# A decoder MLP in split float32: operand rows loaded in place, part sums left in two tiles, another order at the stage changes

## The chip, the core and the metric

The kernel runs on one core of a Trainium2 chip. The metric is device time in microseconds, the median of several executions; one further execution was profiled, and every row below comes from that one. The engines: TensorE (PE, the matrix engine), VectorE (DVE), ScalarE (ACT), GpSimd (POOL) and SyncE (SP). Here SP only issues DMAs, and POOL after the first third of the kernel does nothing else either.

## The reference, cut to what is computed

One layer of a decoder over 576 rows (512 prompt rows and 8x8 sample rows). The part that the change touches is the second half, `finish_layer`:

```python
D_MODEL = 2048; D_FF = 4 * D_MODEL
def finish_layer(x, attn, conv_y, pe, ...):
    ...
    x = x + jnp.concatenate([attn, conv_y], axis=-1) @ w_out
    hid = jnp.square(jax.nn.relu(rms_norm(x, g_mlp) @ w_up))
    x = x + hid @ w_down
    gate = jax.nn.sigmoid(rms_norm(x, g_ple) @ w_ple_gate)
    return x + (pe @ w_ple) * gate
```

All of it is float32. The kernel splits each operand into a high part in a shorter format (`float32r`) and a low part, the rest, and makes a product from three matmuls: high by high, high by low, low by high.

## The kernel before

**Layout and stages.** Features lie on the 128 partitions, rows along the free axis (`NR` = 576, `HR` = 288 is half). The first 925 us are the input projection, attention and convolution, which the change leaves alone. Then come the output projection (`outproj`, 16 tiles of 96 matmuls), the up projection, the down projection, the gate and a short end.

**The quad.** Up, down and gate run over *quads*: one 256x256 block of weights against one slot of operands. Up and down use a fast 2x2 block product: 7 products in place of 8 (`PRODS`), each of three matmuls of 288 columns, so 21 matmuls in a quad (lines 1415 to 1421). The order of the products in a quad is 0, 5, 6, 4, 1, 2, 3, and each has a PSUM bank of its own (`pr[i]`); of the eight banks one is spare, so a new segment's second product needs the bank of the old segment's product 0, its third that of product 5, and so on.

**Weights.** `QStream` loads two quads' weights at a time (`w2r`, 512 KB, three buffers, on SP's queue), DVE makes three block sums of them (lines 1613 to 1615), ACT rounds the seven blocks to the high part (`w2h`) and DVE subtracts for the low part (`w2l`), three buffers each. `prep(q)` is called two quads ahead. On DVE the first block sum of the *next* load stands ahead of this quad's `w2l`.

**Operand slots.** A slot holds the seven operand blocks of 128x288 in high and low form (`xs`: `[128, 2, 7, 288]`, a ring of eight). The raw blocks lie in DRAM (`up_in`, `down_in`, tensors `ui` and `di`); `slot_loads` fetches them in two DMAs (432 and 576 KB) into the two buffers of a staging tile `ro`, and `slot` lets ACT write the high part from `ro` and DVE the low part. The slots 0, 1 and 7 of the up projection are made straight from the output projection (`split7`).

**Segments.** A segment is one output tile's run of quads. Up has 32 segments of 8 quads. Down goes in rounds over its 8 output tiles (`plan`): in the first round the tiles take 3, 3, 3, 4, 5, 6, 7 and 8 quads, later 7 each. After a segment the seven products are combined to the tile `c` (`combine_head`, `combine_tail`: 2 copies on ACT, 6 operations on DVE). A down segment that isn't the tile's last one adds its `c` to `x1` in DRAM by an accumulating DMA from POOL (line 1290). `c` has two buffers. `fin_up` scales, applies ReLU and squares an up tile, makes its blocks (`tsums`) and stores them to `down_in`.

**What sets the order.** The engines' programs are in the order in which the code writes them. `Beside` holds two queues of generators that do the work beside the matmuls: queue 0 the finishing work (`fins`), queue 1 the slots. `run` steps them on a credit in us per quad, with queue 0 ahead of queue 1; `flush` and `flush_all` force them. `mk(g, j)` puts the making of slot j on queue 1; a table of hooks calls it at the quad after which the slot's place in the ring was last read.

**Ahead of the up projection.** Before the first quad the code flushes slots 2, 3 and 4 (`bg.flush(slots[1, j].work)`), so their splits stand on ACT and DVE ahead of the weights of quad 2. `prep(0)` and `prep(1)` were called in the last tile of the output projection. `fin_out(p)` finishes a pair of output projection tiles: scaled copy `cg`, blocks `T`, the stores to `up_in`, and then the squares for the norm (`sq`); `cg`, `T` and `sq` share two buffers (tag `b`).

## Time and profile before

| What | Value |
|---|---|
| median of 3 runs | 2873.62 us (2868.43 to 2873.94) |
| profiled execution, its time | 2875.02 us |
| profiled execution, its span | 2873.2 us |
| PE busy | 2730.2 us (95%) |
| DVE busy | 2061.0 us (72%) |
| ACT busy | 1176.8 us (41%) |
| mean granted TensorE clock | 0.978 |
| HBM read and written | 431.53 MB and 95.55 MB |

How to read the rows that follow. A row of the windows view names a stretch in us from the span's start and gives its length, then for PE, PEld (the weight load), DVE, ACT and POOL the busy time with the number of instructions in brackets, then the granted TensorE clock, the share of the DMA engines that was busy, and GB/s. A timeline row has start, duration, engine, line, operation, output and inputs, and in square brackets the idle time ahead of it with what ended that wait. Matmuls are pipelined, so one lasts about 0.29 us while the next starts 0.13 us later. A group row gives count, busy time and mean ns of one. A waits row gives total, times and longest.

### The profile page before, as it was taken

To read this page: it belongs to the slowest core of one execution; us is meant where nothing else is said; L and a number is where in the kernel's file an instruction comes from. 1 tells how busy PE (TensorE), PEld (TensorE's weight loads), DVE (VectorE), ACT (ScalarE), POOL (GpSimd) and SP (SyncE) were. 2 spreads that over 40 slices of the span, in tenths; PEclk is the share of its full clock that TensorE was granted. 3 is DMA by queue.
4 is the path that set the end of the run, shared out by engine and by line. 5 is a ranking of instruction groups with operands and counts; after the bars stand their busy time and mean duration, and the time that the engine had idled before them with its cause. 6 is when DMAs were issued, how large, how long until landed. Compare 5 with 4: busy or idle time off the path is not lost.

```text
span 2873.2 us, 56874 instructions
## 1 busy us (share of the span) xinstructions
PE 2730.2 (95%) x22165; PEld 2624.0 (91%) x22165; DVE 2061.0 (72%) x3613; ACT 1176.8 (41%) x1755; POOL 396.0 (14%) x702
## 2 busy tenths in 40 slices
PE   7999999999999998899999999989999999998996
PEld 7888888898787997899999999989999999998996
DVE  5577766766644434788888888888887888897444
ACT  4232233345633323444444444444444444444332
POOL 1167755741100000000000000000000000000000
PEclk9999999999999999999999999999999999999998
DMA  4599888988745444444444444466665656555445
GB/s 147 173 276 288 268 276 267 286 279 299 257 140 173 145 159 160 129 136 138 141 147 144 137 135 145 154 193 185 159 184 144 180 163 175 167 178 182 156 149 176
DMA packets 243536, 530.81 MB, mean 185 GB/s; under 512 B 25793, under 2 KB 31170, under 8 KB 243266
## 3 DMA queue, kind: packets, MB, share of 16 engines
q1 hardware_dynamic: 197330, 422.72, 45.5%
q10 hardware_dynamic: 33552, 60.87, 7.1%
q0 software_dynamic: 12384, 43.58, 6.5%
q8 instruction: 174, 2.85, 0.4%
q14 instruction: 96, 0.79, 0.1%
HBM read 431.53 MB, written 95.55 MB: 183 GB/s over the span
## 4 chain that ended last, share of the span: by engine, by line
PE 63%; DVE 5%; DMA 3%; ACT 2%; issue 2%; SPq 0%; DVEq 0%; ACTq 0%
PE P L1420 16%; PE P L1419 16%; PE P L1421 15%; PE U L463 7%; PE P L1458 2%; PE P L1460 2%; PE P L1459 2%; PE U L1074 1%; DVE w2l L152 1%; DMA ro<-di 1%; DMA ui<-cg 1%; ACT xs L149 1%; DMA ro<-ui 1%; DVE xs L152 0%; ACT sq L1215 0%
## 5 line engine op out<-in xcount | busy, mean ns | idle before, releaser
L1419 PE MATMUL P<-xs,w2h 128*128 128x288 f32 x3584 | 1069.1, 298 | 35.7 <-ACT w2h L149 11.3
L1420 PE MATMUL P<-xs,w2h 128*128 128x288 f32 x3584 | 1068.1, 298 | 4.0 <-DVE xs L152 4.0
L1421 PE MATMUL P<-xs,w2l 128*128 128x288 f32 x3584 | 1064.5, 297 | 6.0 <-DVE w2l L152 6.0
L149 ACT ACTIVATE w2h<-w2r 128x896 fp32r<-128x896 f32 (+1 forms) x576 | 523.3, 915 | 771.8 <-PE P L1420 471.1
L152 DVE TENSOR_TENSOR w2l<-w2r,w2h 128x896 fp32r<-128x896 f32 (+1 forms) x576 | 600.3, 1042 | 175.8 <-ACT w2h L149 174.0
L1419 PEld LDWEIGHTS P<-xs,w2h 128*128 128x128 f32 x3584 | 680.9, 190 | 42.2 <-ACT w2h L149 11.8
L1421 PEld LDWEIGHTS P<-xs,w2l 128*128 128x128 f32 x3584 | 680.0, 190 | 7.9 <-DVE w2l L152 7.8
L1420 PEld LDWEIGHTS P<-xs,w2h 128*128 128x128 f32 x3584 | 681.9, 190 | 5.5 <-DVE xs L152 5.2
L463 PE MATMUL U<-xh,whi 128*128 128x288 f32 x1792 | 405.1, 308 | 11.0 <-ACT whi L123 10.1
L463 PE MATMUL U<-xh,wlo 128*128 128x288 f32 x1792 | 387.5, 298 | 9.2 <-DVE wlo L129 9.2
L463 PE MATMUL U<-xl,whi 128*128 128x288 f32 x1792 | 386.7, 298 | 2.3 <-DVE xl L298 1.2
L463 PEld LDWEIGHTS U<-xh,whi 128*128 128x128 f32 x1792 | 291.1, 191 | 32.7 <-issue 17.1
L463 PEld LDWEIGHTS U<-xh,wlo 128*128 128x128 f32 x1792 | 291.1, 190 | 11.1 <-DVE wlo L129 11.1
L463 PEld LDWEIGHTS U<-xl,whi 128*128 128x128 f32 x1792 | 291.2, 191 | 3.2 <-DVE xl L298 1.7
L123 ACT ACTIVATE whi<-wraw 128x512 fp32r<-128x512 f32 x224 | 141.0, 630 | 295.0 <-PE U L463 162.6
L1290 POOL DMA_DIRECT2D x<-c x32 | 27.6, 861 | 1565.9 <-DVE c L1531 1565.9
L129 DVE TENSOR_TENSOR wlo<-wraw,whi 128x512 fp32r<-128x512 f32 x224 | 159.3, 712 | 113.0 <-ACT whi L123 110.3
L1613 DVE TENSOR_TENSOR w2r<-w2r 128x512 f32<-128x512 f32 (+1 forms) x272 | 177.9, 654 | 48.7 <-DMA w2r<-in_w_up 24.9
L984 DVE SCALAR_TENSOR_TENSOR y<-ue,cv,y 128x512 f32<-128x512 f32 x240 | 183.4, 764 | 4.2
L985 POOL TENSOR_SCALAR cvt<-us,cv 128x64 f32<-128x64 f32 x240 | 166.5, 694 | 21.6
L1458 PE MATMUL P<-xs,w2h 128*128 128x288 f32 x512 | 152.8, 298 | 0.1
L1459 PE MATMUL P<-xs,w2h 128*128 128x288 f32 x512 | 152.4, 298 | 0.0
(331 smaller groups left out, 2981.6 us busy)
## 6 DMA issues: line engine op xcount, KB each, us to landing
k<-in_cache_kv SPq DMA_DIRECT2D x256, 256.0 KB, 5.2
v<-in_cache_kv SPq DMA_DIRECT2D x256, 256.0 KB, 5.0
w2r<-in_w_up SPq DMA_DIRECT2D x128, 512.0 KB, 4.0
w2r<-in_w_down SPq DMA_DIRECT2D x112, 512.0 KB, 4.3
wraw<-in_w_main ACTq DMA_DIRECT2D x160, 256.0 KB, 5.4
di<-T SPq DMA_DIRECT2D x32, 576.0 KB, 4.2
ro<-di SPq DMA_DIRECT2D x32, 576.0 KB, 5.6
x<-c POOLq DMA_DIRECT2D x32, 576.0 KB, 6.1
```

The lines of the kernel that those rows point to most:

```text
L129: self.nc.vector.tensor_tensor(lo, self.raw.pop(c), f(hi), ALU.subtract)
L149: self.nc.scalar.activation(out, in_, AF.Copy, **kw)
L152: self.nc.vector.tensor_tensor(out, in_, f(hi), ALU.subtract)
L463: self.nc.tensor.matmul(u[:, r, :HR], w, x[:, r * HR:(r + 1) * HR], start=first and n == 0, stop=last and n == 2)
L984: nc.vector.scalar_tensor_tensor(y, ue[:, j:j + NPR], w, y, ALU.mult, ALU.add)
L985: nc.gpsimd.tensor_scalar(t, us[:, :, j:j + 8], w, None, ALU.mult)
L1419: nc.tensor.matmul(o, hi[:, ia, :], s.hi[:, ib, :], start=(k == k0), stop=False)
L1420: nc.tensor.matmul(o, hi[:, ia, :], s.lo[:, ib, :], start=False, stop=False)
L1421: nc.tensor.matmul(o, lo[:, ia, :], s.hi[:, ib, :], start=False, stop=(k == k1 - 1))
L1458: nc.tensor.matmul(o, hi[:, ia, :], s.hi[:, kh, rows], start=first and kh == 0, stop=False)
L1459: nc.tensor.matmul(o, hi[:, ia, :], s.lo[:, kh, rows], start=False, stop=False)
L1613: lambda: V(w[:, :, 4:6, :], w[:, :, 0:1, :].broadcast_to([128, m, 2, 128]), w[:, :, 1:3, :], ALU.add),
```

## The change

It does five things.

1. **Slots load in place.** For up and down, `mk` now issues one DMA (128x2016, all seven blocks) into the low half of the slot itself, at once and not when the slot's work is reached; `slot` rounds from there to the high half and subtracts in place. The gate's slots do the same within their work. Only slot 2 of the up projection still comes through `ro` (`slot_early`).
2. **Part sums leave in two tiles.** A down segment that isn't a tile's last makes `c` without the products 1, 2 and 3 (`part_head`: one copy on ACT, four operations on DVE), and ACT copies those three products to a tile `e` (`part_tail`). POOL adds `e` to `x1` and then `c`.
3. **First up segment.** Slots 2 to 6 are no longer flushed ahead of the first quad but one each after quads 0 to 4; three weight loads and `prep(0)` to `prep(2)` stand in the last output projection tile, where two stood.
4. **`fin_out`** writes the squares ahead of the operands (except for the last pair).
5. **First gate segment**: queue 0 isn't flushed one quad before its end any more, only at the end.

**Where rows move.** First ACT, from the end of the output projection into the up projection (`whi` are output projection weights, `w2h` the new weights, `xs` slots, `cg` and `T` the last output pair). Before:

```order
L123 ACTIVATE whi<-wraw 128x512 x4
L149 ACTIVATE w2h<-w2r 128x896 x2
L149 ACTIVATE xs<-ro 128x864
L149 ACTIVATE xs<-ro 128x1152
L149 ACTIVATE xs<-ro 128x864
L149 ACTIVATE xs<-ro 128x1152
L149 ACTIVATE xs<-ro 128x864
L149 ACTIVATE xs<-ro 128x1152
L149 ACTIVATE w2h<-w2r 128x896 x2
L1237 ACTIVATE cg<-c,vecs 128x576 x2
```

and now:

```order
L123 ACTIVATE whi<-wraw 128x512 x4
L149 ACTIVATE w2h<-w2r 128x896 x3
L1236 ACTIVATE cg<-c,vecs 128x576 x2
L149 ACTIVATE xs<-cg 128x288
L149 ACTIVATE xs<-cg 128x576
L149 ACTIVATE xs<-T 128x1152
L149 ACTIVATE xs<-ro 128x864
L149 ACTIVATE xs<-ro 128x1152
L149 ACTIVATE w2h<-w2r 128x896
L149 ACTIVATE xs<-xs 128x864
L149 ACTIVATE xs<-xs 128x1152
```

The weights of the third quad moved ahead of all slots, the last output pair ahead of slot 2, and between two slots there is now one quad's weights.

Second, DVE at the same place (`wlo` is the low part of output projection weights, `w2r` the block sums, `c<-U,rx` the eviction of an output projection tile). Before:

```order
L1118 TENSOR_TENSOR c<-U,rx 128x576
L129 TENSOR_TENSOR wlo<-wraw,whi 128x512 x2
L1613 TENSOR_TENSOR w2r<-w2r 128x2x256
L1614 TENSOR_TENSOR w2r<-w2r 128x2x128
L1615 TENSOR_TENSOR w2r<-w2r 128x2x128
L1613 TENSOR_TENSOR w2r<-w2r 128x2x256
L152 TENSOR_TENSOR w2l<-w2r,w2h 128x896
L1614 TENSOR_TENSOR w2r<-w2r 128x2x128
L1615 TENSOR_TENSOR w2r<-w2r 128x2x128
L152 TENSOR_TENSOR w2l<-w2r,w2h 128x896
L1118 TENSOR_TENSOR c<-U,rx 128x576
```

and now:

```order
L1117 TENSOR_TENSOR c<-U,rx 128x576
L129 TENSOR_TENSOR wlo<-wraw,whi 128x512
L1653 TENSOR_TENSOR w2r<-w2r 128x2x256
L1654 TENSOR_TENSOR w2r<-w2r 128x2x128
L1655 TENSOR_TENSOR w2r<-w2r 128x2x128
L1653 TENSOR_TENSOR w2r<-w2r 128x2x256
L152 TENSOR_TENSOR w2l<-w2r,w2h 128x896
L1654 TENSOR_TENSOR w2r<-w2r 128x2x128
L129 TENSOR_TENSOR wlo<-wraw,whi 128x512
L1655 TENSOR_TENSOR w2r<-w2r 128x2x128
L152 TENSOR_TENSOR w2l<-w2r,w2h 128x896
L1653 TENSOR_TENSOR w2r<-w2r 128x2x256
```

The last `wlo` of the output projection moved behind the sums of the first two weight loads.

Third, SP from the last up segment into the down projection (`di_126` and so on are the raw blocks of one slot each, `di_153` the store of an up tile, 512 or 2x512 a load of one or two quads' weights). Before:

```order
L1598 DMA w2r<-in_w_down 128x2x512
L1246 DMA di_153<-c 128x288
L1247 DMA di_153<-c 128x576
L1248 DMA di_153<-T 128x1152
L1493 DMA ro<-di_123 128x864
L1493 DMA ro<-di_123 128x1152
L1598 DMA w2r<-in_w_down 128x512
L1493 DMA ro<-di_124 128x864
L1493 DMA ro<-di_124 128x1152
L1598 DMA w2r<-in_w_down 128x2x512
L1493 DMA ro<-di_125 128x864
L1493 DMA ro<-di_125 128x1152
```

and now, behind the slots `di_123` to `di_125` and the first two quads' weights:

```order
L1247 DMA di_153<-T 128x1152
L1345 DMA xs<-di_126 128x2016
L1638 DMA w2r<-in_w_down 128x512
L1345 DMA xs<-di_127 128x2016
L1345 DMA xs<-di_128 128x2016
L1638 DMA w2r<-in_w_down 128x2x512
L1345 DMA xs<-di_129 128x2016
L1345 DMA xs<-di_130 128x2016
L1638 DMA w2r<-in_w_down 128x512
L1638 DMA w2r<-in_w_down 128x2x512
```

All eight slots' loads now stand within the last up segment, one per quad, with the weights of the third quad behind four of them and those of the sixth behind all eight.

**The diff:**

```diff
@@ -184,7 +184,6 @@
 
     heads = 0
     draining = False
-    loaded = None
     later = []
 
 
@@ -1133,12 +1132,12 @@
             for _ in gen:
                 bg.spend(EL(512) / 2)
                 if n == KT - 1 and h == 0:
-                    self.W.dma(0)
-                    self.W.dma(1)
+                    for i in range(3):
+                        self.W.dma(i)
                 if n == KT - 1 and h == 5:
-                    self.loaded = self.slot_loads(self.up_in[2])
-                if n == KT - 1 and h in (4, 6):
-                    bg.spend(self.W.prep(h // 2 - 2))
+                    self.early = self.slot_early(self.up_in[2])
+                if n == KT - 1 and h in (2, 4, 6):
+                    bg.spend(self.W.prep(h // 2 - 1))
                 bg.run(8 * n + h, 1.6)
                 h += 1
             if n % 2 and n < KT - 1:
@@ -1250,6 +1249,8 @@
     def fin_out(self, p, c):
         nc = self.nc
         nc.sync.dma_start(self.x1[p], c)
+        if p < 7:
+            yield from self.squares(p, c)
         cg, T = yield from self.operands(c, self.g_mlp[:, 2 * p:2 * p + 2])
         if p in (0, 1, 7):
             s = self.xslot() if p < 2 else self.last
@@ -1258,8 +1259,8 @@
             h.hi, h.lo = s[:, 0], s[:, 1]
         else:
             self.stored(cg, T, self.up_in[p])
-        yield from self.squares(p, c)
         if p == 7:
+            yield from self.squares(p, c)
             yield from self.norm(self.P_)
 
     def phase2(self):
@@ -1287,6 +1288,9 @@
         def fin_down(p, c, r, final):
 
             if not final:
+                c, e = c
+                quarters = self.x1[p].rearrange("p a (b n) -> p (a b) n", b=2)
+                nc.gpsimd.dma_start(quarters[:, :3, :], e[:, :3, :], accum_op=ALU.add)
                 nc.gpsimd.dma_start(self.x1[p], c, accum_op=ALU.add)
                 yield 0
                 return
@@ -1326,27 +1330,37 @@
         segs, W, slots, fin_of = self.segs, self.W, self.slots, self.fin_of
         fins = (None, fin_up, fin_down, fin_gate)
 
-        def mk(g, j, s=None):
+        def mk(g, j, early=None):
 
             h = slots[g, j] = Slot()
+            t = self.xslot()
+            h.hi, h.lo = t[:, 0], t[:, 1]
+            src = (self.up_in, self.down_in, self.x2)[g - 1][j]
+            if g == 3:
+                h.hi, h.lo = (x.rearrange("p a n -> p (a n)")[:, :2 * NR].rearrange("p (a n) -> p a n", a=2)
+                              for x in (h.hi, h.lo))
+
+            def load():
+                bg.flush(fin_of[g - 1, j])
+                nc.sync.dma_start(f(h.lo), src)
+
+            if g < 3 and not early:
+                load()
 
             def build():
-                bg.flush(fin_of[g - 1, j])
-                t = s or self.xslot()
-                h.hi, h.lo = t[:, 0], t[:, 1]
+                if g == 3:
+                    load()
+                if not early:
+                    yield -2
                 if g < 3:
-                    yield from self.slot(t, (self.up_in, self.down_in)[g - 1][j], EL)
+                    yield from self.slot(t, early)
                     return
-                h.hi, h.lo = (x.rearrange("p a n -> p (a n)")[:, :2 * NR].rearrange("p (a n) -> p a n", a=2)
-                              for x in (t[:, 0], t[:, 1]))
-                r = t2.tile([128, 2, NR], F32, name="ro", tag="ro", bufs=2)
-                nc.sync.dma_start(r, self.x2[j])
-                yield -2
                 for i in range(2):
                     gv = self.g_ple[:, 2 * j + i:2 * j + i + 1]
-                    self.split_hi(h.hi[:, i, :], r[:, i, :], scale=gv)
-                    nc.vector.scalar_tensor_tensor(h.lo[:, i, :], r[:, i, :], gv, f(h.hi[:, i, :]), ALU.mult, ALU.subtract)
-                yield 2 * EL(NR)
+                    r = f(h.lo[:, i, :])
+                    self.split_hi(h.hi[:, i, :], r, scale=gv)
+                    nc.vector.scalar_tensor_tensor(h.lo[:, i, :], r, gv, f(h.hi[:, i, :]), ALU.mult, ALU.subtract)
+                    yield EL(NR)
 
             h.work = bg.add(1, build())
 
@@ -1377,12 +1391,10 @@
                 again[p] = y
 
         hook(lastuse[3, 5], reload)
-        ss = [self.xslot() for _ in range(2, 8)]
-        self.last = ss[5]
-        for j in range(2, 7):
-            mk(1, j, ss[j - 2])
-        for j in range(2, 5):
-            bg.flush(slots[1, j].work)
+        mk(1, 2, self.early)
+        for j in range(3, 7):
+            mk(1, j)
+        self.last = self.xslot()
         fin_of[0, 7] = bg.add(0, self.fin_out(7, self.oc_))
         slots[1, 7] = Slot()
         slots[1, 7].work = fin_of[0, 7]
@@ -1393,6 +1405,9 @@
                 pg, ppr, c, r, pfinal, pp_ = prev
                 if pg == 3:
                     cost = self.plain_end(ppr, c, rb)
+                elif pg == 2 and not pfinal:
+                    c = c, self.part_tail(ppr)
+                    cost = 0
                 else:
                     cost = self.combine_tail(ppr, EL)
                     c = c[0]
@@ -1421,18 +1436,25 @@
                     nc.tensor.matmul(o, lo[:, ia, :], s.hi[:, ib, :], start=False, stop=(k == k1 - 1))
             for fn in hooks.get(t, ()):
                 fn()
-            if k == k1 - 2:
-                if si:
-                    bg.flush_all(0)
+            slow = k0 == 0 and p == 0 and g != 2
+            if k == k1 - 2 and not slow:
+                bg.flush_all(0)
                 r = pre[g](p, lastseg[g, p] == si)
             bg.run(1000 + t, 3.18 if g == 3 else 2.79)
+            if g == 1 and p == 0 and 2 <= k + 2 < 7:
+                bg.flush(slots[1, k + 2].work)
             if k == k1 - 1:
-                if si:
+                if g != 1 or p:
                     bg.flush_all(0)
+                if slow:
+                    r = pre[g](p, lastseg[g, p] == si)
                 if before:
                     bg.flush(before)
                 if g == 3:
                     c = t2.tile([128, 2, NR], F32, name="c", tag="c", bufs=2)
+                elif g == 2 and lastseg[g, p] != si:
+                    c = self.part_head(pr)
+                    bg.spend(4 * EL(HR))
                 else:
                     c = self.combine_head(pr)
                     bg.spend(2 * EL(HR))
@@ -1486,23 +1508,22 @@
             self.split_lo(l, src, h)
             yield EL(n)
 
-    def slot_loads(self, src):
+    def slot_early(self, src):
+
         parts = []
         for i, n in ((0, 3), (3, 4)):
             r = self.t2.tile([128, 4, HR], F32, name="ro", tag="ro", bufs=2)
             self.nc.sync.dma_start(r[:, :n], src[:, i:i + n, :])
-            parts.append((i, n, r))
+            parts.append(r)
         return parts
 
-    def slot(self, s, src, EL):
+    def slot(self, s, early=None):
+
         hi, lo = s[:, 0], s[:, 1]
-        parts, self.loaded = self.loaded, None
-        if not parts:
-            parts = self.slot_loads(src)
-            yield -2
-        for i, n, r in parts:
-            self.split_hi(hi[:, i:i + n, :], r[:, :n])
-            self.split_lo(lo[:, i:i + n, :], r[:, :n], hi[:, i:i + n, :])
+        for i, n in ((0, 3), (3, 4)):
+            r = early[i // 3][:, :n] if early else f(lo[:, i:i + n, :])
+            self.split_hi(hi[:, i:i + n, :], r)
+            self.split_lo(lo[:, i:i + n, :], r, hi[:, i:i + n, :])
             yield EL(n * HR)
 
     def combine_head(self, pr):
@@ -1518,6 +1539,25 @@
         nc.scalar.activation(wt[:, 1, :], q(4), AF.Copy)
         pr["c"] = c, wt
         return c, wt
+
+    def part_head(self, pr):
+
+        V = self.nc.vector.tensor_tensor
+        q = lambda i: pr[i][:, :HR]
+        c = self.t2.tile([128, 2, NR], F32, name="c", tag="c", bufs=2)
+        c11, c12, c21, c22 = c[:, 0, :HR], c[:, 0, HR:], c[:, 1, :HR], c[:, 1, HR:]
+        self.nc.scalar.activation(c11, q(0), AF.Copy)
+        V(c12, c11, q(5), ALU.subtract)
+        self.nc.vector.scalar_tensor_tensor(c21, c12, -1.0, q(6), ALU.mult, ALU.subtract)
+        V(c22, c21, q(4), ALU.add)
+        V(c12, c12, q(4), ALU.subtract)
+        return c
+
+    def part_tail(self, pr):
+        e = self.t2.tile([128, 4, HR], F32, name="e", tag="ro", bufs=2)
+        for j, (i, sign) in enumerate(((1, 1.0), (2, 1.0), (3, -1.0))):
+            self.nc.scalar.activation(e[:, j, :], pr[i][:, :HR], AF.Copy, scale=sign)
+        return e
 
     def combine_tail(self, pr, EL):
         nc = self.nc
```

## The prediction

> **What bounds the kernel now.** I read the windows view first, for the stretches in which PE falls behind, then the waits, then the timelines of PE and of what it waits for. Four stretches, with their lengths, PE's busy time and its matmuls:
>
> ```profile
> 1400.00:1600.00 200.00, 200.00 (x1503) 200.00 (x1502) 172.19 (x269) 93.20 (x108) 0.00 (x0) 1.00 0.44 141
> 1128.50:1220.00 91.50, 69.70 (x445) 66.89 (x444) 66.80 (x106) 40.38 (x47) 0.00 (x0) 0.85 0.43 133
> 1860.00:1960.00 100.00, 86.43 (x585) 83.40 (x585) 87.77 (x137) 48.23 (x59) 4.35 (x5) 0.91 0.72 207
> 1960.00:2500.00 540.00, 533.50 (x3985) 530.88 (x3984) 457.02 (x723) 244.61 (x292) 23.21 (x27) 1.00 0.62 169
> ```
>
> The first row is the plateau: PE never rests, 200/1503 = 0.1331 us a matmul, 2.79 us a quad of 21. Nothing the change does to ACT or DVE can shorten that; what can be won is what the other stretches lose against it. The start of up loses 91.5 - 445 x 0.1331 = 32.3 us, the turn from up to down 100 - 585 x 0.1331 = 22.1, the rounds of down 540 - 3985 x 0.1331 = 9.6. Part of a loss is idle time, part the clock (0.85, 0.91 in two rows). The waits that end last there:
>
> ```profile
> 1077.08 0.53 PE L463 MATMUL U<-xh,wlo 128*128 128x288 f32 x2 [0.88 <-DVE wlo L129]
> 1139.90 0.61 PE L1419 MATMUL P<-xs,w2h 128*128 128x288 f32 x1 [11.08 <-ACT w2h L149]
> 1873.11 0.40 PE L1421 MATMUL P<-xs,w2l 128*128 128x288 f32 x1 [1.26 <-DVE w2l L152]
> 1889.19 0.61 PE L1420 MATMUL P<-xs,w2h 128*128 128x288 f32 x1 [1.14 <-DVE xs L152]
> 1907.22 0.61 PE L1419 MATMUL P<-xs,w2h 128*128 128x288 f32 x1 [4.23 <-ACT c L1515]
> 1945.46 0.40 PE L1419 MATMUL P<-xs,w2h 128*128 128x288 f32 x1 [2.03 <-ACT c L1515]
> 2007.52 0.40 PE L1419 MATMUL P<-xs,w2h 128*128 128x288 f32 x1 [1.25 <-ACT c L1515]
> ```
>
> ACT itself waited there for loads into the two `ro` buffers, or for a buffer:
>
> ```profile
> 1073.67 1.17 ACT L1215 ACTIVATE sq<-c 128x1152 f32<-128x1152 f32 x1 [3.36 <-DMA ui<-cg]
> 1128.39 0.92 ACT L149 ACTIVATE xs<-ro 128x864 fp32r<-128x864 f32 x1 [3.35 <-DMA ro<-ui]
> 1137.85 1.16 ACT L149 ACTIVATE xs<-ro 128x1152 fp32r<-128x1152 f32 x1 [3.27 <-DMA ro<-ui]
> 1138.92 1.77 ACT L149 ACTIVATE w2h<-w2r 128x896 fp32r<-128x896 f32 x2
> 1998.89 1.17 ACT L149 ACTIVATE xs<-ro 128x1152 fp32r<-128x1152 f32 x1 [2.34 <-DMA ro<-di]
> ```
>
> So the 11.08 us gap is no lack of work: quad 2's weights stand on ACT behind three slots, which wait for their loads.
>
> **Output projection, squares first: -5.9 us.** The squares wait 3.36 us for the store of `cg`, whose buffer they take, and `whi` and `wlo` stand behind them. Five pairs are stored (2 to 6).
>
> ```profile
> ACT sq L1215 <- DMA ui<-cg: 16.7, 5, 3.4
> PE U L463 <- DVE wlo L129: 5.8, 7, 1.1
> PE U L463 <- ACT whi L123: 1.5, 5, 0.3
> ```
>
> Ahead of `cg` the squares find a buffer whose last user was a pair earlier, two tiles of 96 matmuls or 26 us ago. What is left is 1.17 us of squares, which the 3.36 covers twice. Of the 7.3 us of PE waits the five pairs hold about 0.88 + 0.3 each: -5.9. Bounds 0 and -7.3.
>
> **Start of up: -14 us.** Quad 2 no longer waits for three slots, but DVE has all their work to do still, in the same segment. So I follow DVE from the last eviction to the first combine of segment 0, which stands at 1172.60 now:
>
> ```profile
> 1116.34 0.69 DVE L1613 TENSOR_TENSOR w2r<-w2r 128x512 f32<-128x512 f32 x1 [1.58 <-DMA w2r<-in_w_up]
> 1118.93 0.69 DVE L1613 TENSOR_TENSOR w2r<-w2r 128x512 f32<-128x512 f32 x1 [0.97 <-DMA w2r<-in_w_up]
> 1123.27 0.76 DVE L1118 TENSOR_TENSOR c<-U,rx 128x576 f32<-128x576 f32 x1 [0.85 <-PE U L463]
> 1172.60 0.45 DVE L1516 TENSOR_TENSOR c<-c,P 128x288 f32<-128x288 f32 x1
> L152 DVE TENSOR_TENSOR w2l<-w2r,w2h 128x896 fp32r<-128x896 f32 x510 | 554.0, 1086 | 87.9 <-ACT w2h L149 86.8
> L1613 DVE TENSOR_TENSOR w2r<-w2r 128x512 f32<-128x512 f32 x238 | 163.2, 686 | 46.1 <-DMA w2r<-in_w_down 23.2 <-DMA w2r<-in_w_up 22.3
> L1615 DVE TENSOR_TENSOR w2r<-w2r 128x256 f32<-128x256 f32 x238 | 100.8, 424 | 6.4
> L1531 DVE TENSOR_TENSOR c<-c,t 128x576 f32<-128x576 f32 x72 | 54.6, 758 | 2.5
> L152 DVE TENSOR_TENSOR xs<-ro,xs 128x1152 fp32r<-128x1152 f32 x36 | 48.8, 1354 | 18.3 <-ACT xs L149 18.3
> L152 DVE TENSOR_TENSOR xs<-ro,xs 128x864 fp32r<-128x864 f32 x36 | 37.9, 1053 | 10.0 <-ACT xs L149 10.0
> L1528 DVE TENSOR_TENSOR c<-P,c 128x288 f32<-128x288 f32 x72 | 32.3, 449 | 1.0 <-PE P L1421 1.0
> ```
>
> The moved sums cost first: the last `wlo` now stands behind block sums that wait for weights which land at 1116.3 and 1118.9. It ends at 1118.9 + 0.69 + 1.09 + 0.42 + 0.7 = 1121.8. The last tile's fourth chunk needs it about 1120.3 (its eviction at 1123.3 less 2.9 us of matmuls): +1.3 us, bounds 0 and 3. The eviction begins when two more `w2l` and their sums are done, near 1125. Then on DVE: eviction 0.76; the last pair's blocks and low halves, 0.76 + 3 x 0.45 + 0.76 + 1.35 = 4.2; five slots of 1.05 + 1.35, 12.0; seven `w2l`, 7.6; three sums of 0.69 and seven of 0.42, 5.0; two additions of the norm, 1.5. That is 31.1, so the combine stands at 1156 instead of 1172.6, 16 us earlier, and PE's segment ends with it. The bound is now DVE: 4.26 us a quad for quads 2 to 6 (slot 2.41, `w2l` 1.09, sums 0.76) against PE's 2.79, in stalls of about 1 us. Stalls this close cost clock once at 1889 (the 0.61 us matmul); I take one such spell, 2.5 us beyond DVE's pace: -14. Bounds: -19 if all eight quads run at PE's pace but for quad 2, -7 if the segment stays at half clock (21 x 0.24 = 5.04 us a quad).
>
> The Trainium skill, "TensorE: Matmul & The Clock Gate", section "What's actually happening", says that the clock halves after one idle window of about 3.4 us and that this window runs free of the kernel's own timing. By that, stalls of 1 us might cost nothing, or, by the window's phase, a spell; the gap ahead of 1889.19 (1.14 us after another of 2 us) fits its second half.
>
> **Turn from up to down: 0 us, from two sides.** For the change: the loads of slots 0 and 1 no longer wait for `ro`, so the 1.26 us at 1873.11 goes; slots 3 to 7 lie ready early, so the wait at 1945.46 goes with its cold spell (3.6 us lost in the 20 us around it); each part segment saves DVE 3.0 - 4 x 0.45 = 1.2 us. About -5. Against it stand the loads' order and the pair of additions:
>
> ```profile
> 1115.00:1120.00 5.00, 5.00 (x39) 5.00 (x39) 2.61 (x5) 1.80 (x2) 0.00 (x0) 1.00 0.96 323
> 1880.00:1900.00 20.00, 16.48 (x99) 15.68 (x99) 16.66 (x30) 6.83 (x10) 0.93 (x1) 0.83 0.56 156
> 1940.00:1960.00 20.00, 17.88 (x123) 17.30 (x122) 18.81 (x27) 10.85 (x13) 0.85 (x1) 0.91 0.69 207
> w2r<-in_w_down SPq DMA_DIRECT2D x112, 512.0 KB, 4.3
> x<-c POOLq DMA_DIRECT2D x32, 576.0 KB, 6.1
> 1903.13 1.35 DVE L1279 TENSOR_TENSOR c<-c,rb 128x1152 f32<-128x1152 f32 x1
> ```
>
> All eight loads of 128 x 2016 x 4 = 1.03 MB stand on SP within the last up segment, and the sixth down quad's weights behind them: 8.26 MB of slots and some 2.2 MB of weights and stores pass first. At full load the DMA engines move 323/0.96 = 335 GB/s, so 31 us, plus 2 for the landing. They start when quad 0 of that segment is done, 7 quads or 19.5 us ahead of the first down quad: the weights land 13.5 us behind its start. On DVE their block sum stands ahead of slot 2's second low part, which quad 2 of down needs 6 to 10 us in. So that low part ends 13.5 + 0.4 + 1.1 + 0.3 + 1.35 = 16.7 us in, and quad 2, with most of its matmuls at half clock (18 x 0.24), near 21. Now it ends near 1894 (20 matmuls at half clock behind 1889.19), 18 us after the turn at 1876 (1873.11 and 20 matmuls); with the next quad's start still at half clock, +4. The second: `c` of the first part segment is free after two DMAs in a row, about 5 + 6.1 us and two issues; the second segment's combine (now held until 1907 by the finishing of the last up tile, 1903.13 and on) takes that buffer next, about 1 us later than ACT is ready: +1. Sum 0. Bounds -8 (weights in time, all stalls but 1907's gone) and +10 (loads at 250 GB/s).
>
> The page "DMA: Bandwidth & Descriptors" of the Trainium skill, section "Measured (HBM→SBUF, 128 partitions, SWDGE, issued from GpSimd)", has 425 GB/s for 16 MB. At that rate the same bytes would take 24 us, an estimate, and the late weights would cost nothing: the time would be near 2842. No stretch of this trace moves that much.
>
> **Rounds of down: -6.5 us.** The wait at 2007.52 has behind it ACT's 2.34 us for a second `ro` load, which had to wait for the buffer. In place there is no such wait, and DVE has 1.2 us less a segment of 19.5. Of the 9.6 us I keep 3, for slot loads of 3.1 us ahead of weights on SP that also wait for PE's quad. ACT's added copies (4 of 0.4 us where there were 2) end 0.4 us after the segment, under ACT's wait for `w2h` buffers; `e` adds 432 KB per segment to DMA engines 62% busy. Bounds -9.6 and +3.
>
> **Gate: 0.** PE's order is unchanged, and the moved flush has the norm at the same matmul.
>
> Sum: -5.9 - 14 + 0 - 6.5 = -26.4 on 2875.0 us, the profiled execution's own time, which lies 1.4 us above the median of the runs: 2848.6 there, 2847 as a median.
>
> **The rivals.** *Late weights* at the turn (+10): 2857. For it: DVE waits for `w2r` loads already (46.1 us). *Half clock* through the first up segment (+7): 2854. For it: clock 0.85 there now. Against it: of the waits worked out above none is longer than 1.5 us. *Weights in time* (-8): 2839; for it, that the stall needs a queue strictly in order, which no row of this trace shows; against it, the median of 4.3 us to landing, more than twice the 1.6 us that 512 KB take at 335 GB/s, so loads do wait in line. *Slower*: the same queue, but at the rate that the turn moves now, 156 GB/s over 1880 to 1900. Then 10.4 MB take 67 us instead of 31, PE stands for the 36 more, and -26 + 36 gives 2883. It decides from a rate below some 180 GB/s on, where 10.4 MB take 27 us more. Against it: at 1880 the share was only 0.56, the queue was waiting for buffers, not bytes. *Gains given back*: only the squares' gain shows, DVE's backlog moves on into later segments and the turn costs 3: 2871. Against it: on the plateau DVE is busy 172 of 200 us, so a backlog is worked off there without PE waiting.
>
> **How the numbers follow.** Forecast 2847 with chance 0.50, its own range 2838 to 2856; late weights 0.15; half clock 0.10; weights in time 0.10; slower 0.09; given back 0.06. The range 2835 to 2864 leaves out the last two and the edges. 0.2% is 5.7 us, about what a measurement tells from no change: faster 0.85, same 0.06, slower 0.09.
>
> **What would show it.** No wait of `sq` for `ui<-cg`; PE's first long gap gone, 445 matmuls in about 75 us and DVE without idle time behind the last eviction; the wait for `wlo` near 1120 there; the sixth down quad's weights landing well behind the turn with DVE waiting ahead of a block sum; no ACT wait for slot loads in the rounds. It is wrong if PE stands over 5 us in a piece at the turn, or if DVE's waits for `w2r` in the rounds grow beyond now's.

## The result and the profile after

The changed kernel takes 2868.89 us (median of 20 runs, 2861.30 to 2875.17) against 2866.79 us of the kernel before in the same session (2861.38 to 2877.03): a ratio of 1.0004, 95% interval [0.9993, 1.0015]. No change, where 2847 us was forecast. The profiled execution took 2869.06 us, its span is 2867.1 us.

So 26 us were either not won or were given back. The windows view of the changed kernel has the plateau, the first up segment, a piece of the turn to the down projection, and the rounds of down between two TensorE waits that both kernels have (columns as before: length, busy time of PE, PEld, DVE, ACT and POOL with their instructions, granted clock, DMA share, GB/s):

```profile
1400.00:1600.00 200.00, 200.00 (x1502) 200.00 (x1501) 171.57 (x269) 94.12 (x108) 0.00 (x0) 1.00 0.44 140
1122.00:1195.00 73.00, 65.94 (x463) 62.77 (x463) 65.04 (x105) 39.19 (x46) 0.00 (x0) 0.98 0.49 166
1840.00:1860.00 20.00, 16.81 (x113) 16.21 (x112) 16.65 (x26) 9.69 (x12) 0.00 (x0) 0.92 1.01 400
1985.30:2482.20 496.90, 478.75 (x3528) 471.18 (x3529) 380.60 (x594) 231.82 (x306) 41.25 (x48) 1.00 0.73 183
```

The same rounds in the kernel before:

```profile
2009.48:2486.18 476.70, 472.35 (x3529) 470.34 (x3529) 404.75 (x642) 216.08 (x258) 20.62 (x24) 1.00 0.61 169
```

The two pairs of ends tell where the time went. The rounds begin at 1985.30 instead of 2009.48, 24.2 us early, and end at 2482.20 instead of 2486.18, 4.0 us early: the same 3,528 matmuls took 20.2 us more. The gain was there, and the rounds gave most of it back. (The changed kernel's profile reaches the output projection 2.4 us later, at 908.32 instead of 905.93, behind stages that the change leaves alone; counted from there the gain up to the rounds is 26.6 us.) TensorE stands 18.2 us in the rounds (496.90 - 478.75) instead of 4.4; the rest of the 20.2 are matmuls that last longer behind a stop (0.40 us and not 0.29 in the rows below).

The waits views of those rounds, VectorE, ScalarE and TensorE, first of the kernel before (2009 to 2500):

```profile
DVE w2r L1613 <- DMA w2r<-in_w_down: 21.3, 23, 2.4
DVE xs L152 <- ACT xs L149: 5.6, 3, 2.4
ACT xs L149 <- DMA ro<-di: 6.6, 5, 2.6
PE P L1419 <- DVE c L1516: 3.8, 4, 1.0
```

and of the changed one (1985 to 2480):

```profile
DVE w2r L1653 <- DMA w2r<-in_w_down: 39.1, 27, 2.9
DVE xs L152 <- ACT xs L149: 38.0, 18, 3.7
ACT xs L149 <- DMA xs<-di: 45.4, 19, 4.0
PE P L1434 <- DVE c L1550: 9.1, 12, 1.0
PE P L1436 <- DVE w2l L152: 5.1, 11, 1.0
SPq L1345 <- PE P L1436: 46.2, 21, 3.2
```

ScalarE stands 45 us until operand rows have landed, for 19 of 21 loads, in 18 cases with VectorE behind it. TensorE stands at 12 segment ends for `c`, 9.1 us in all and never over 1.0 us at once, and 5.1 us for the low part of the weights. One segment in the timelines of the changed kernel, ScalarE, VectorE and TensorE, and SP's issue of the load:

```profile
2025.78 0.34 SPq L1345 DMA_DIRECT2D xs<-di  x1
2032.96 1.98 ACT L149 ACTIVATE xs<-xs 128x864 fp32r<-128x864 f32 x2 [3.50 <-DMA xs<-di]
2033.92 2.41 DVE L152 TENSOR_TENSOR xs<-xs 128x864 fp32r<-128x864 f32 x2 [3.14 <-ACT xs L149]
2041.33 0.69 DVE L1653 TENSOR_TENSOR w2r<-w2r 128x512 f32<-128x512 f32 x1 [1.40 <-DMA w2r<-in_w_down]
2044.73 0.45 DVE L1550 TENSOR_TENSOR c<-c,P 128x288 f32<-128x288 f32 x1
2045.23 0.40 PE L1434 MATMUL P<-xs,w2h 128*128 128x288 f32 x1 [0.84 <-DVE c L1550]
```

and the same split in the kernel before:

```profile
2047.16 0.90 SPq L1493 DMA_DIRECT2D ro<-di  x2
2053.81 1.97 ACT L149 ACTIVATE xs<-ro 128x864 fp32r<-128x864 f32 x2
2055.15 2.32 DVE L152 TENSOR_TENSOR xs<-ro,xs 128x864 fp32r<-128x864 f32 x2
```

There the load was issued 6.65 us ahead of the split, and ScalarE found the rows. Now ScalarE is ready at 2029.46 (2032.96 less the 3.50), 3.7 us after the issue, and waits. The load into its place starts only when TensorE has last read the place: 46.2 us of waits for TensorE on SP for 21 loads, 2.2 us each. The splits stand where they stood, two quads behind the load's place in the program.

The change did a second thing to the rows: it made one load out of two. The issues in the rounds, with the median time from issue to landing, first of the kernel before, then of the changed one:

```profile
ro<-di SPq DMA_DIRECT2D x21, 432.0 KB, 3.6
ro<-di SPq DMA_DIRECT2D x21, 576.0 KB, 5.6
xs<-di SPq DMA_DIRECT2D x21, 1008.0 KB, 6.2
```

The first split used to need the 432 KB alone, 3.6 us behind the issue; now it needs the whole slot, 6.2 us behind it. Two quads of 2.79 us are 5.6 us, so 2.2 us of waiting and 6.2 us of landing come too late by some 2.8 us (an estimate from these medians; ScalarE's 19 waits are 2.4 us each). No run loads a slot in place in two pieces, so the two reasons are not told apart by a run of their own.

### The profile page after: what moved, and what is told of

Same layout as the page of the kernel before. It is cut to its first block, busy times and chain, and to the rows that moved or that the text cites. A ratio compares the mean times of both kernels' runs of the same rounds, so it can differ in the third digit from the quotient of the medians.

```text
span 2867.1 us, 56846 instructions
## 1 busy us (share of the span) xinstructions
PE 2727.2 (95%) x22165; PEld 2614.3 (91%) x22165; DVE 2026.0 (71%) x3549; ACT 1194.7 (42%) x1819; POOL 427.1 (15%) x734
## 3 DMA queue, kind: packets, MB, share of 16 engines
q1 hardware_dynamic: 192146, 422.72, 45.4%
## 4 chain that ended last, share of the span: by engine, by line
PE 70%; DVE 11%; DMA 11%; issue 3%; ACT 2%; SPq 1%; DVEq 0%; ACTq 0%
PE U L462 18%; PE P L1434 12%; PE P L1435 12%; PE P L1436 12%; DVE w2l L152 3%; DMA v<-in_cache_kv 3%; DMA xs<-di 3%; PE P L1480 2%; DMA w2r<-in_w_down 2%; PE P L1482 2%; PE P L1481 2%; PE S L804 1%; DVE xs L152 1%; PE O L825 1%; DMA wraw<-in_w_main 1%
## 5 line engine op out<-in xcount | busy, mean ns | idle before, releaser
L1293 POOL DMA_DIRECT2D x<-e x32 | 27.6, 861 | 1372.0 <-DMA w2r<-in_w_down 969.7
```

## The experiments

The theories after this reading: the second adding DMA makes the weights late (A); the in-place load holds SP's queue, with the weights behind it (B); the new order of the part sum makes VectorE late (C). Each run was timed beside the kernel before, whose median lay between 2866.79 and 2870.97 us from one set of runs to the next: a difference between medians of two sets can be off by some 4 us, and the ratios compare better.

**One part undone each time.** `one_sum` takes the branches with `part_head` and `part_tail` out of the loop and the addition of `e` out of `fin_down`:

```diff
-                elif pg == 2 and not pfinal:
-                    c = c, self.part_tail(ppr)
-                    cost = 0
...
-                elif g == 2 and lastseg[g, p] != si:
-                    c = self.part_head(pr)
-                    bg.spend(4 * EL(HR))
```

> The changed kernel with its part 2 undone: a part sum of the down pass again leaves as one tile c in one adding DMA, combined on VectorE by six operations as before; everything else of the change stays (squares first, early weights, operand rows loaded into their places). Theory A (the second adding DMA: 432 KB more per part segment, so the weight loads land later, 5.7 us against 4.1 us in the same stretch of a round, and VectorE stands at a block sum): the 18 us that the rounds lost come back, the time is 2846 to 2853 us, ratio to before 0.993 to 0.995, and TensorE's waits for c at the ends of part segments are gone. Theory B (operand rows loaded in place wait on SP's queue for TensorE and hold up the weight loads behind them): the rounds lose as much as in the changed kernel, 2866 to 2872 us, ratio 0.999 to 1.002. Theory C (order: VectorE comes to the first subtraction of c late for reasons of the new sequence of the part sum alone): as A in time.

2868.06 us, ratio 1.0006 [0.9989, 1.0023]. A and C fall as sole causes: with one tile and the old combination the loss is all there (the same rounds take 499.86 us in its profile).

`no_e` leaves out one line:

```diff
-                nc.gpsimd.dma_start(quarters[:, :3, :], e[:, :3, :], accum_op=ALU.add)
```

> The changed kernel with one adding DMA left out: the tile e is still computed by ScalarE, but never added to the row sums, so products 1, 2 and 3 of the part segments are missing from the output. Nothing in the order of the engines changes. Theory A (traffic of the second adding DMA): 2844 to 2853 us, weight loads in the rounds land in about 4.2 us again, the waits for c at segment ends fall under 3 us in all. Theory B (in-place loads on SP's queue): unchanged, 2866 to 2872 us. Theory C (the new order of the part sum on VectorE and ScalarE): unchanged too, 2866 to 2872 us.

2856.71 us, 0.9966 [0.9950, 0.9981]. Between the theories: about 12 us hang on that DMA. Against `one_sum`, which moves the same bytes, it is 11 us faster, what VectorE's shorter part sum is worth where rows are late.

`start_only` is `one_sum` with the rows of down through `ro`:

```diff
-            if g < 3 and not early:
+            if g == 1 and not early:
                 load()
...
+                if g == 2:
+                    bg.flush(fin_of[g - 1, j])
+                    parts = self.slot_early(src)
```

> The changed kernel with part 2 undone and the operand rows of the down pass loaded through two ro tiles as before; what stays is the start: squares first in the output projection, three weight loads and three preparations before the up pass, in-place rows of the up pass. All three theories: the gain at the start (22 us in the profile of the changed kernel) is kept to the end, 2842 to 2849 us, ratio 0.991 to 0.994. If the rounds still lose 10 us or more, none of the theories holds, and the loss comes from how the earlier start meets the rounds.

2845.85 us, 0.9924 [0.9902, 0.9945], as expected: 0.8% faster than the kernel before. Its rounds in the windows view:

```profile
1983.29:2459.59 476.30, 472.23 (x3529) 470.36 (x3529) 405.47 (x642) 216.11 (x258) 20.64 (x24) 1.00 0.61 169
```

476.30 us, what the kernel before takes. The start's gain reaches the end.

`late_slots` issues the in-place loads two quads later:

```diff
-            if g < 3 and not early:
+            if g == 1 and not early:
                 load()
...
-                if g == 3:
+                if g == 2:
+                    yield -2
+                if g > 1:
                     load()
                 if not early:
...
```

> The changed kernel with each in-place load of the down pass issued two quads later, so that on SP's queue it stands behind one or two weight loads more and the quad that last reads the place is over when its turn comes; both adding DMAs stay. Theory B (SP stands in an in-place load and holds up the weights): the loss in the rounds goes, 2846 to 2854 us, SP's waits for TensorE at these loads fall to near nothing. Theory A (traffic) and theory C (order of the part sum): 2862 to 2872 us, waits for c at segment ends stay near 11 us.

2868.99 us, 1.0004 [0.9990, 1.0018]. B falls: SP's wait is gone and nothing came back. Its waits, of SP and ScalarE:

```profile
SPq L1345 <- PE P L1438: 3.7, 7, 1.6
ACT xs L149 <- DMA xs<-di: 38.3, 18, 3.7
```

The split moved along with the load, two quads behind it as before, so the rows were late as before. They were so without any wait for TensorE worth naming: these loads take 7.6 us (median) to land, and two quads are 5.6 us. The reading at the time was theory D: the splits come due before a load that must wait for TensorE can land. This run shows that the wait is not needed for it; the landing of the whole slot alone is longer than two quads.

**In-place rows alone, and the splits moved.** `inplace_only` puts the loads into the kernel before:

```diff
+            if g == 2:
+                s = self.xslot()
+                bg.flush(fin_of[g - 1, j])
+                nc.sync.dma_start(f(s[:, 1]), self.down_in[j])
...
+                if g == 2:
+                    yield -2
...
```

> The kernel before with one part of the change alone: the operand rows of the down pass are loaded straight into their places when TensorE has last read them, with the splits two quads later as in the changed kernel; start, order and part sums as before. Theory D: the rounds lose 18 to 24 us against the kernel before, 2885 to 2892 us, ratio 1.006 to 1.009, with VectorE waiting about 30 us for xs in the rounds. If the loss needs the earlier start or the new order (a drift that meets a bound of the DMA or of VectorE further on): 2866 to 2874 us.

2894.55 us, 1.0085 [1.0060, 1.0110]: the ratio is in D's range, the time 2.6 us above it, and the other reading falls. Its rounds and VectorE's wait:

```profile
2001.91:2502.96 501.05, 485.58 (x3528) 476.19 (x3529) 405.26 (x642) 214.35 (x258) 20.63 (x24) 0.99 0.59 161
DVE xs L152 <- ACT xs L149: 31.0, 18, 3.4
```

501.05 - 476.70 = 24.4 us, with the old start and the old part sums: neither is needed for the loss.

The next five change one number, the quads between the load and its splits, two of them on top of `one_sum`. The first, `split4`:

```diff
                 if not early:
-                    yield -2
+                    yield -4 if g == 2 else -2
```

> The changed kernel, whole, with one number different: in the down pass the two splits of an in-place row set are due four quads after its load is issued, not two (11.2 us of TensorE work instead of 5.6). Theory D (the load into its place can start only when TensorE has last read the place, while the splits stand where they stood before; ScalarE stands 45 us in the rounds until the rows land, VectorE 38 us behind it, and what VectorE does late is the combination at the end of the part segment): the waits of VectorE for xs fall under 8 us in the three rounds, the waits for c at segment ends go, the time is 2842 to 2850 us, ratio 0.991 to 0.994. Theory A2 (the second adding DMA slows the weight loads, and that alone costs 12 us): only part comes back, 2855 to 2860 us. Theory B (SP's queue held by the in-place load): nothing changes, 2866 to 2872 us, as the loads stand at the same places on SP's queue.

> As the run before in this set, but with a part sum of the down pass in one tile and one adding DMA, combined by six operations of VectorE: in-place rows with splits four quads after the load. Theory D: 2842 to 2850 us, within 0.2% of the run with two tiles, as VectorE has room for the six operations once it no longer stands for rows. Theory A2: 2843 to 2850 us here and some 12 us more with two tiles. Theory B: 2866 to 2872 us.

> The changed kernel with the splits of the in-place rows of the down pass due six quads after their load (16.7 us of TensorE work). Theory D: the load has landed either way, so the same time as with four quads within 0.2%, 2842 to 2850 us; a segment has seven quads, so the splits now fall near the segment's end and could collide with the part sum there, at most 3 us per round turn. Theory A2: 2855 to 2860 us. Theory B: 2866 to 2872 us.

| Quads | whole change | with one tile |
|---|---|---|
| 2 | 2868.89, 1.0004 | 2868.06, 1.0006 |
| 3 | 2856.49, 0.9956 [0.9939, 0.9973] | 2854.29, 0.9955 [0.9938, 0.9973] |
| 4 | 2858.86, 0.9949 [0.9930, 0.9967] | 2883.08, 1.0051 [1.0033, 1.0068] |
| 6 | 2872.99, 1.0007 [0.9994, 1.0020] | not run |

Four quads take every wait of VectorE for rows away, as D said, but the time missed D's range and lies in A2's, and with one tile it is worse than with two quads, which no theory had. Six quads missed every range but lie nearest to B's, which `late_slots` had ruled out. VectorE and TensorE with four quads and one tile:

```profile
DVE w2r L1644 <- DMA w2r<-in_w_down: 56.1, 23, 5.1
PE P L1428 <- DVE c L1528: 15.1, 19, 1.0
```

The 2.4 us of splits now end some 4 us ahead of the part sum's operations, and TensorE waits for `c` 19 times; with two tiles the part sum is shorter, and these waits stay under 3 us in all with four quads and come back with six (11.8 us). That this crowding is the cause is argued and not shown: in the whole change VectorE's waits for weights grow too with the later splits, from 25.7 us with three quads to 50.9 with four and 82.8 with six (1985 to 2480).

> The changed kernel with the splits of the in-place rows of the down pass due three quads after their load is issued. Runs so far: two quads 2869 us (VectorE stood 38 us in the rounds for rows), four quads 2859 us (no wait for rows left, but the splits then come right before the part sum at the segment's end), six quads 2873 us (splits and part sum collide, 12 us of waits for c). Theory D with this crowding: three quads cost the least of the four, since the longest wait for rows was 3.7 us and one quad is 2.79 us, and the splits end two quads before the part sum: 2846 to 2855 us, VectorE's waits for xs under 10 us, TensorE's waits for c in the rounds under 4 us. Theory A2 (the second adding DMA alone sets some 12 us through late weights): 2857 to 2861 us. If the crowding were nothing, and the four-quad loss came from the turn or the weights: 2858 us or more.

> In-place rows with splits three quads after the load, and a part sum in one tile with one adding DMA (six operations of VectorE). With two quads this combination took 2868 us, with four 2883 us. Theory D with crowding: no waits for rows, but the six operations of the part sum and the splits of 2.4 us stand in the same seven quads, two quads apart; 2850 to 2866 us, more than the run with two tiles by 2 to 11 us. Theory A2: 2843 to 2849 us, less than the run with two tiles by about 10 us.

Three quads missed D's first range by 1.5 us and hit its second in time, though not the 2 to 11 us that one tile was to take more. With one tile and with two the time is the same, so the second DMA alone (A2) doesn't set it.

**The second adding DMA, with rows through `ro`.** `start_two_sums` is the whole change with the rows as in `start_only` and `e` in a buffer of tag `b`; the second run leaves the DMA of `e` out.

```diff
-        e = self.t2.tile([128, 4, HR], F32, name="e", tag="ro", bufs=2)
+        e = self.t2.tile([128, 2, NR], F32, name="e", tag="b", bufs=2).rearrange("p a (b n) -> p (a b) n", b=2)
```

> The version with the start alone (2846 us, rows of the down pass through ro) plus the part sums in two tiles, e in one of the two work buffers that the rounds leave free, with the second adding DMA. The prediction's term for the rounds (6.5 us for VectorE's shorter work at the segment ends): 2838 to 2841 us. Theory E (traffic takes back what the shorter work gives, whatever the rows do): 2844 to 2850 us, with the waits for weights from the DMA longer than in the start-only version (18.9 us in the rounds there). Theory A2 (the second adding DMA costs 12 us and the shorter work gives only where VectorE is late): 2852 to 2860 us.

> The same with the second adding DMA left out, so that products 1, 2 and 3 of the part segments are missing from the output; e is still computed. The prediction's term: the same as with it, 2838 to 2841 us. Theory E: 2834 to 2841 us, 8 us or more below the run with it. Theory A2: 2844 to 2848 us, as the start-only version, since TensorE waited only 5 us in its rounds in all, and 12 us below the run with it.

2865.11 us, 0.9986 [0.9972, 0.9999], and without that DMA 2843.89 us, 0.9915 [0.9892, 0.9938]. The 21 us between them are the price of the second adding DMA, above what any theory gave; the shorter part sum brings some 2 us (2845.85 to 2843.89), which the intervals don't tell from nothing. Waits and DMA issues of `start_two_sums` in the rounds:

```profile
DVE w2r L1657 <- DMA w2r<-in_w_down: 40.2, 27, 3.5
DVE xs L152 <- ACT xs L149: 22.2, 20, 3.4
ro<-di SPq DMA_DIRECT2D x21, 576.0 KB, 7.8
```

against 18.9 and 4.6 us of the same waits and 5.6 us to landing in `start_only`. In the first round, whose part segments are short, TensorE waits 2.78 and 3.35 us for ScalarE's copy into `c` at 1905 and 1924, 1.38 and 0.85 us without the DMA. The copy stands on ScalarE right behind a split that waits for its rows, 1.68 us here and 1.76 us at 1924 (0.51 and 0.45 without the DMA):

```profile
1903.51 1.16 ACT L149 ACTIVATE xs<-ro 128x1152 fp32r<-128x1152 f32 x1 [1.68 <-DMA ro<-di]
1904.58 0.39 ACT L1553 ACTIVATE c<-P 128x288 f32<-128x288 f32 x1
```

So both parts end in waits of the same kind, and the last two runs ask through which of them `e` acts: splits three quads behind the loads, with two adding DMAs and with one.

> Start alone plus part sums in two tiles with both adding DMAs, rows through ro, and the splits of the rows due three quads after their loads (2865 us with two). Theory F (the second adding DMA costs its 19 us because the row loads land later, 7.8 us against 5.6, than the splits come due): VectorE's waits for xs in the rounds fall from 22 to under 8 us and at least half of the 19 us comes back, 2846 to 2856 us. Theory G (it costs them because the weight loads land later, 4.6 us against 4.3, whatever the rows do): 2861 to 2869 us, waits for weights from the DMA stay near 40 us.

> The control: start alone, one adding DMA, rows through ro, splits due three quads after their loads. VectorE hardly waits for rows with two quads (4.6 us in the rounds), so the move can gain nothing there: 2843 to 2850 us if the later splits are harmless; 2851 to 2858 us if splits one quad nearer to the part sum cost about 8 us by themselves, which would also be what the in-place rows lose with three quads (2856 us).

2869.60 us, 1.0007 [0.9994, 1.0020], and 2857.49 us, 0.9960 [0.9945, 0.9975]. F falls: the waits for rows are gone and the time didn't come back, while VectorE's waits for weights stay at 37.2 us (17.6 in the control), as G has it; the time is 0.6 us above G's range. With no wait for rows in the rounds `e` still costs 2869.60 - 2857.49 = 12 us. In the two profiles the price falls half in the first round of down, which takes 134.43 us against 127.51, and half in what follows up to the gate, 642.77 against 635.15. In that first round VectorE waits 14.1 us for weights (6.4 in the control), and ScalarE once 2.9 us until an adding DMA frees a `c`. So `e` acts mainly through other things than the rows; that it is the weights alone, and that the rest of the 19 to 21 us goes through the rows, is not shown.

The control says something else: moving the splits by one quad costs 11.6 us where nobody waits for rows. In it TensorE stands at each round's turn, here at one of three:

```profile
2133.83 0.40 PE L1434 MATMUL P<-xs,w2l 128*128 128x288 f32 x1 [2.74 <-DVE w2l L152]
2138.23 0.61 PE L1432 MATMUL P<-xs,w2h 128*128 128x288 f32 x1 [3.21 <-DVE c L1532]
```

The stop has weights behind it that come late. VectorE stands just ahead of it for a block sum, and SP's waits for the two `ro` buffers, which the splits free, have grown (second row; 8.6, 3, 2.9 in `start_only`):

```profile
2132.09 0.69 DVE L1648 TENSOR_TENSOR w2r<-w2r 128x512 f32<-128x512 f32 x1 [5.79 <-DMA w2r<-in_w_down]
SPq L1511 <- DVE xs L152: 18.0, 6, 5.2
```

By this trace, two slots are loaded close together at a round's turn. The second slot's loads wait on SP for the buffers, later by the quad that the splits moved, and the next weights stand behind them in SP's program. With in-place rows there is no such buffer, yet with three quads VectorE stands 3.09 and 4.35 us for weights at the same turn (one tile and two); why is not shown.

And 2857.49 us is what the in-place rows take with three quads and one tile (2854.29): at equal due times of three quads loading in place costs nothing that these runs can tell. Its price in the changed kernel is that it can't meet the two quads, and three are dear for another reason.

**The start's two halves**, each undone in `start_only`, the squares in one run and the third weight load with its `prep` in the other:

```diff
-        if p < 7:
-            yield from self.squares(p, c)
...
-                    for i in range(3):
-                        self.W.dma(i)
+                    self.W.dma(0)
+                    self.W.dma(1)
...
```

> The version with the start alone (2846 us), its output projection with the squares of a piece after the operands again, as in the kernel before. By the term of the prediction for squares first (5.9 us, all of it TensorE's waits for squares at the output projection): 2851 to 2853 us. If those waits are hidden or paid elsewhere: 2844 to 2848 us.

> The version with the start alone (2846 us) with two weight loads and two preparations before the up pass instead of three, as in the kernel before; the operand rows of the up pass stay in place. By the prediction's term for the start of up (14 us for weights and rows together, the weight wait of 11.1 us the largest in it): 2855 to 2860 us. If the third preparation is worth nothing and the order of the rows carries the gain: 2844 to 2849 us.

2851.86 us, 0.9940 [0.9919, 0.9960]: 6.0 us slower without squares first, though the intervals overlap. The profiles agree: the output projection takes 217.66 us without and 211.39 us with them. With two weight loads 2848.34 us, 0.9932 [0.9909, 0.9955]: the third is worth 2.5 us by the medians, less than can be told from nothing. Its profile shows more: the first up segment takes 44.45 us instead of 29.23, and the second round of down begins 7.8 us later, as half of the loss comes back in the next up segments. So that the order of the rows alone carries the start is not shown.

## Why the prediction was wrong

- **Plateau**: right, 1502 matmuls in 200 us.
- **Squares first, -5.9 us**: right in size, 6.0 us in the run that undoes it and 6.3 us of output projection in its profile (4.2 us between the kernel before and the change). The wait for `wlo` that the moved sums cause was put at 1.3 us near 1120 and is 0.94 us:

```profile
1118.55 0.54 PE L462 MATMUL U<-xh,wlo 128*128 128x288 f32 x2 [0.94 <-DVE wlo L129]
1128.65 0.40 PE L1435 MATMUL P<-xs,w2h 128*128 128x288 f32 x1 [1.15 <-DVE xs L152]
1177.25 0.40 PE L1436 MATMUL P<-xs,w2l 128*128 128x288 f32 x1 [1.63 <-DVE w2l L152]
1129.50:1133.00 3.50, 3.09 (x13) 3.09 (x14) 3.50 (x5) 3.50 (x5) 0.00 (x0) 0.54 1.01 387
```

- **Start of up, -14 us**: right in kind, too small. The wait at 1177.25 stood at 1199.67 before, 22.4 us later, where the two terms gave 19.9; counted from the first matmul of the output projection it is 24.8 us. The first up segment alone takes 29.23 us instead of 50.18, 21 us less, beyond the bound of -19. The cold spell that I had put at 2.5 us came: behind stops of 1.15 and 0.60 us the granted clock is 0.54 over 3.5 us, with 13 matmuls where the plateau has 26 (last row above), some 1.5 us by an estimate from the 0.24 us between these matmuls. In `start_only` the same two stops stand in the first segment and its granted clock is 1.00. The rival of half clock through the whole segment fell, with 0.94 over it (0.76 before). The Trainium skill ("TensorE: Matmul & The Clock Gate", "What's actually happening") has the clock halve after an idle window of about 3.4 us that runs free of the kernel's timing. That the spell came in one profile and not in the other fits a free-running window; but TensorE stood for 1.75 us only, so the spell came with less idle time than the page names.
- **Turn, 0 us**: right as a sum. From the wait for `c` at 1879.79 (1855.63 now) to the rounds' start it took 129.69 us and now 129.67 (2009.48 and 1985.30 at the end). The terms in it were off: the loads moved 400 GB/s at a full share, not 335, so the slower rival at 156 GB/s fell. The Trainium skill's 425 GB/s ("DMA: Bandwidth & Descriptors", "Measured (HBM→SBUF, 128 partitions, SWDGE, issued from GpSimd)") is nearer than my estimate. The kernel before had such a stretch too, which I overlooked: 416 GB/s from 9 to 19 us. Weights did come late, VectorE waited 11.4 us for them from 1840 to 1985 (0.7 us before, from 1860 to 2009), but the turn took no longer, so the rival of late weights fell as a price. That the turn's sum came out exact with its terms off is luck. No stop of TensorE there was over 5 us; the longest was 4.32 us, for `c`.
- **Rounds of down, -6.5 us with bounds -9.6 and +3**: this is the step that failed; they lost 20.2 us. Three sentences of it were wrong. "In place there is no such wait": I took the wait for the `ro` buffer away. That the loads "also wait for PE's quad" I had, but priced it only as a delay of the weights behind them on SP, the 3 us kept. A staging tile lets the load run while TensorE still reads the old rows; in place it starts after the last read, and it lands as one piece. I did not set this wait and landing (2.2 and 6.2 us) against the two quads (5.6 us) in which the splits come due. 45.4 us of ScalarE's waits and 24 us of time alone (`inplace_only`) stand there. "`e` adds 432 KB per segment to DMA engines 62% busy" was costed at nothing; alone it costs 19 us (`start_two_sums` less `start_only`). And the 1.2 us of VectorE saved per segment could win little, as TensorE waited only some 4 us there; with the rows through `ro` and without the DMA of `e` it won some 2 us. The two losses don't add, 20.2 us together: with rows late, the shorter part sum is worth what the second DMA costs (11 against 12 us, from `one_sum`, `no_e` and the change).
- **The signs** that I had named did show it: a wait of ScalarE for slot loads in the rounds, and waits for `w2r` grown from 21.3 to 39.1 us. The rival *gains given back* had the right time, 2871, by luck, and the wrong mechanism: VectorE carried no backlog out of the start, whose whole gain was still there at 1985.

Left open: why the weights come late at the round turns in the in-place kernels with three quads, how the 19 us of `e` divide between rows, weights and the free `c`, and how much of the rows' lateness in place is the single load.

## What to carry to other kernels

A staging buffer is also a head start: before loading straight into a place, set the last read of the place plus the landing time of the piece that the first consumer needs against the point at which the first consumer stands in its program, and move that point or keep the buffer. An extra transfer on engines with idle share is not free where other loads' landing times are what someone waits for: look at the medians to landing, not at the share. And when several edits go together, undo each alone: here the edits to the start were worth 24 us, and the two to the rounds took them back.

## What the runs showed of the hardware

Adding DMAs took 1.8 times as much DMA engine time per byte as loads here. The queues of the kernel before and of the change between 1985 and 2470 (packets, MB, share of 16 engines' span):

```profile
q1 hardware_dynamic: 29860, 68.16, 44.3%
q0 software_dynamic: 3521, 14.46, 17.4%
```

```profile
q1 hardware_dynamic: 25326, 64.31, 41.8%
q0 software_dynamic: 6828, 24.46, 31.1%
```

That is 1.20% per MB for the adding queue (`software_dynamic`) and 0.65% for the loads, and 1.27% and 0.65% with two adding DMAs per segment.
